# A hybrid encoder layer in fp32: a ring of its own for rows loaded ahead, and other ties for the loads of h

## The chip, the cores and the metric

The kernel runs on one core of a Trainium2 chip. Its engines work side by side: TensorE (PE) multiplies, VectorE (DVE), ScalarE (ACT) and GpSimd (POOL) do elementwise work, and SyncE (SP) issues every DMA of this kernel from one in-order queue. The metric is the device time of one execution in microseconds; the median of several runs counts. A lower time is better.

## The reference, cut to what matters

One layer of an encoder with two attention groups runs on 2048 prompt tokens and 32 sample tokens (a decoding step with 128 cached rows), D = 1024, all in fp32:

```
a  = rmsnorm(h)
qa, ka, va, qb, kb, vb = split(a @ w_in)
oa = diff_attn(qa, ka, va)            # 4 heads, two maps each, chunk-causal
ob = band_attn(qb, kb, vb)            # 8 heads of 64, a band of 9 chunks of 64
h  = h + concat(rmsnorm(oa), rmsnorm(ob)) @ w_out
h  = h + square(relu(rmsnorm(h) @ w_up)) @ w_down      # 4096 wide
h  = h + sigmoid(h @ w_ple_gate) * (p @ w_ple_proj)
y  = rmsnorm(h)
```

The outputs are y for both token sets and the new keys and values.

## The kernel before, in words

**Numbers.** Every operand of a product is split into a high and a low part (`split`, L232: ACT copies the high part as fp32r, POOL or DVE subtracts it from the raw value), and `mm3` (L257) makes each product of three matmuls: high x high (L267), high x low (L268), low x high (L269).

**Tokens.** There are four blocks `b` of 512 tokens; block 1 carries the 32 sample tokens as well. `HALVES` pairs the blocks (0, 1) and (2, 3). Between stages, activations lie in HBM: `oT` (attention outputs), `hS` (the residual stream h), `rB` (scales of a norm), `cB` (normed rows), `uS` (operands of the down product).

**Stages in `run` (L1482).** Projections and attention come first. The band attention's second half is followed in the program by `proj_a` (L1581), the projection of group A for blocks 2 and 3, woven by `weave2` (L131) with `onorm` (L840): for each of blocks 0 and 1, `onorm` loads the band outputs, sums their squares, and in a second step makes the norm's scale and stores it to `rB`. `ONP` (L119) says at which units of `proj_a` these two steps are taken: with (first, gap between the blocks, distance), block i steps at units first + i x gap and first + i x gap + distance. `proj_a` has 35 units, 0 to 34.

After that, `outproj` (L878) of blocks 0 and 1 runs. For each of eight column groups d it loads a row of x into a tile `hd`, multiplies, adds, squares it into a tile `tmp`, and stores the new h to `hS`. Woven into block 0's product is `oload(1)` (L853), which loads and splits the attention outputs of block 1 (tile `oraw`). Woven into block 1's product is `norms(0)` (L1603), which ends in `cnorm` (L921): it loads each row of h of block 0 from `hS` (tile `tmp`, by `cload`, L911) and splits it into `cH`, `cL`, the operands of the up product. All of `hd`, `tmp` and `oraw` have the tag `tmp` and share one ring of the pool `wk`, with 3 slots here (`nt`). The class `Mix` (L188) sends a tag to a pool of its own; `oload` and `outproj` load one row ahead when they are given a `Mix` (L862, L883).

The MLP of blocks 0 and 1 follows (`mlp`, L1003). For blocks 2 and 3 the up and down products are done by Strassen's scheme with seven products of half size: `uphase` (L1120) stores its results to `uS`; `dphase` (L1196) runs the seven down products `m` in the order 3, 5, 7, 4, 2, 6, 1. Each has eight steps `c` with two inner steps `k`. A step loads one or two tiles `wd` of w_down (a ring of 8) and a tile `ut` from `uS`, splits `ut` into two tiles `dx` (a ring of 4), makes sums `dv` of two weight tiles where the product wants one, and splits them into `dw`; twelve matmuls per `k` go to four tiles `dp` in PSUM. At the end of a product DVE adds `dp` into tiles of h in SBUF (L1249): product 3 adds into all eight parts of `h[3]`, product 5 into parts 0 to 3 of `h[2]` and `h[3]`. Into `dphase` are woven the gates of blocks 0 and 1 (`gate`, L1284), which load h of a block in one DMA, split it into `hH` and `hL`, load `pn` and gate weights into `wr`, and multiply (`gps`, `pps`).

**Ties.** The tiles h of blocks 2 and 3 (L1696) are loaded by `hmove` (L1622) from `hS` in parts of 128 x 512. So that these loads aren't issued at once, `hstep` (L1699) writes one column of each part from a `dx` tile; the load must wait for that write. `dphase` calls it as `step` (L1233).

**Order.** Each engine's instructions are put in order by a planner, which takes the program's order as priority and a model of the durations, and runs ahead with later instructions where earlier ones aren't ready in its model. On the chip the order is fixed and each engine goes through its own.

Of the kernel before, what the change touches and what calls it, by code (L numbers as in the profile page):

```python
# [12 lines left out]
F32 = mybir.dt.float32  # L13
F32R = mybir.dt.float32r
AF = mybir.ActivationFunctionType
# [29 lines left out]
HALVES = [(0, 1), (2, 3)]  # L45
# [68 lines left out]
OW = 1  # L114
# [1 line left out]
JA0 = [(0, 1), (2, 3, 8)]  # L116
JA1 = [(4, 5), (6, 7)]
JB = [(0, 1), (2, 3, 8), (4, 5), (6, 7)]
ONP = (16, 1, 6)  # L119
ONQ = (8, 1, 1)  # L120
PW = 256
GL = 3
# [4 lines left out]
def drain(gen):  # L127
    for _ in gen:
        pass


def weave2(main, sides, at):
    n = 0
    for _ in main:
        for i, side in enumerate(sides):
            if n in (at[0] + i * at[1], at[0] + i * at[1] + at[2]):
                next(side, None)
        n += 1
    for side in sides:
        drain(side)  # L140


def weave(main, side, step, i=0, n=1):
    for _ in main:
        if i % step == 0:
            for _ in range(n):
                next(side, None)
        i += 1
    drain(side)
# [47 lines left out]
class Kern:  # L197
# [998 lines left out]
    def dphase(self, h, pool, md, step):  # L1196
        nc = self.nc
        def wrow(q, c):
            i, j = int(q[0]) - 1, int(q[1]) - 1
            r = pool.tile([P, 2, 512], F32, tag="wd", bufs=6, name="wd")  # L1200
            self.dma(r.rearrange("p a b -> p (a b)"), self.a["w_down"][8 * j + c, i])
            return r

        def operands(m, sq, so, c):
            ws = [wrow(q, c) for q in sq]
            u = self.rawp.tile([P, 2, 512], F32, bufs=self.nraw, name="ut")
            self.dma(u, self.uS[:, m - 1, 2 * c : 2 * c + 2])
            for k in range(2):
                x = pool.tile([P, 2, 512], F32R, tag="dx", bufs=4, name="dx")
                self.tsplit(x, u[:, k], "dve")  # L1210
                v = ws[0][:, k]
                if len(ws) == 2:
                    v = pool.tile([P, 512], F32, tag="dv", bufs=4, name="dv")
                    nc.vector.tensor_tensor(v, ws[0][:, k], ws[1][:, k], op=so)
                w = self.wp.tile([P, 2, 512], F32R, tag="wc", bufs=self.wtags[2], name="dw")
                self.tsplit(w, v, "dve")
                yield w, x

        add, sub = ALU.add, ALU.subtract
        plan = [  # L1220
            (3, ("11",), add, (("12", add), ("22", add))),
            (5, ("11", "12"), add, (("11", sub), ("12", add))),
            (7, ("12", "22"), sub, (("11", add),)),
            (4, ("22",), add, (("11", add), ("21", add))),
            (2, ("21", "22"), add, (("21", add), ("22", sub))),
            (6, ("21", "11"), sub, (("22", add),)),
            (1, ("11", "22"), add, (("11", add), ("22", add))),
        ]
        for m, sq, so, outs in plan:
            ps = [md.tile([P, 512], F32, tag="mm", name="dp") for _ in range(4)]  # L1230
            for c in range(8):
                for k, (w, x) in enumerate(operands(m, sq, so, c)):
                    if m == 3 and k == 0:  # L1233
                        step(c, x)
                    for d in range(4):
                        sl = slice(P * d, P * d + P)
                        self.mm3(
                            ps[d], [(w[:, 0, sl], w[:, 1, sl], x[:, 0], x[:, 1])],
                            start=c + k == 0, stop=c == 7 and k == 1,
                        )  # L1240
                if c < 7:
                    yield
            adds = [(d, q, op) for d in range(4) for q, op in outs]
            if m == 1:
                adds.sort(key=lambda x: x[1])
            for d, q, op in adds:
                i, t = int(q[0]) - 1, int(q[1]) - 1
                hv = h[2 + t][4 * i + d]
                nc.vector.tensor_tensor(hv, hv, ps[d], op=op)  # L1249
            yield  # L1250
# [231 lines left out]
    def run(self):  # L1482
        tc, nc, a = self.tc, self.nc, self.a
        with ExitStack() as top:

            def opened(stack, name, bufs, space=None, side="left"):
                kw = {} if space is None else {"space": space}
                return stack.enter_context(
                    tc.tile_pool(name=name, bufs=bufs, side=side, reuse_waits="tile", **kw)
                )  # L1490
# [7 lines left out]
            mm = opened(psx, "mm", MM, PSUM)  # L1498
# [11 lines left out]
            with ExitStack() as x:  # L1510
# [10 lines left out]
                wk = opened(x, "setup", 1, side="right")  # L1521
# [59 lines left out]
            def proj_a():  # L1581
                yield from self.proj(HALVES[1], 0, acts, sg, mm, gs=range(GS))
                for b in HALVES[1]:
                    yield from self.proj((b,), 0, acts, sg, mm, vs=(), gs=range(GS, 4))

            weave2(proj_a(), [self.onorm(b, wq, mm, "mm", self.rB) for b in HALVES[0]], ONP)
            s12.close()
# [4 lines left out]
            oa = {}  # L1592
# [8 lines left out]
            wk = opened(sq_, "wk", 1)  # L1601
            acc, cn, st = {}, {}, {}
            def norms(b, act, ps):  # L1603
                r = self.colnorm(acc[b][0], b, 1.0 / D, wk, ps, "mm", None)
                yield
                yield from self.cnorm(b, wk, act, cn, r)

            acc = {b: [] for b in range(4)}
            with ExitStack() as x:
                oq = Sized(opened(x, "oq", 2), BLK, True)  # L1610
                weave(self.outproj(0, wk, oa[0], mm, acc[0]), self.oload(1, wk, oq, oa), 1, 0, OW)
                weave(self.outproj(1, wk, oa[1], mm, acc[1]), norms(0, actq, mm), 1, 1)
            hq = opened(sq_, "hq", 1)
            uq = Sized(opened(sq_, "uq", 10), BLK)
# [7 lines left out]
            def hmove(b, h, load, ds=range(8)):  # L1622
                for d in ds:
                    x, y = h[d][:, : BN[b]], self.hS[:, d, T0[b] : T0[b] + BN[b]]
                    self.dma(*((x, y) if load else (y, x)))
                return h
# [21 lines left out]
            for b in HALVES[0]:  # L1648
                if b == 1:
                    drain(self.cnorm(1, wk, actq, cn))  # L1650
                h = [hq.tile([P, BLK], F32, tag="h", bufs=8, name="h") for _ in range(8)]
                hmove(b, h, True)
                dn = Turn(mm)
                m = self.mlp(b, (h,) + cn[b], wk, uq, mm, dn, (16, 11)[b])
                if b == 0:
# [3 lines left out]
                    def steps(m=m):  # L1659
                        for ch, part in m:  # L1660
                            next(pre, None)
                            if part == 0:
                                yield ch

                    m = steps()
# [30 lines left out]
            h = {b: hh.tile([P, 8, 512], F32, tag="h", name="h") for b in HALVES[1]}  # L1696
            h = {b: [t[:, d] for d in range(8)] for b, t in h.items()}

            def hstep(c, x):  # L1699
                for b in HALVES[1] if c < 4 else ():  # L1700
                    for d in (2 * c, 2 * c + 1):
                        nc.gpsimd.tensor_copy(h[b][d][:, :1], x[:, 0, :1].bitcast(F32))
                    hmove(b, h[b], True, range(2 * c, 2 * c + 2))

            fk = opened(top, "fk", 1)
            udx, gqx = ExitStack(), ExitStack()
# [11 lines left out]
            for i, _ in enumerate(self.dphase(h, ud, md, hstep)):  # L1718
                if i == 48:
                    drain(g)  # L1720
                    gqx.close()
                    left = opened(top, "gx", 1)
                    pair = self.gatepair(h, t3, left, right, md, mg, GL)
                if pair is not None:
                    if 49 < i < 55:
                        next(pair)
                elif i % 4 != 3:
                    next(g, None)
# [68 lines left out]
```

## Time and profile before

| what | value |
|---|---|
| three runs | 2965.36, 2957.69, 2965.66 us |
| median | 2965.36 us |
| profiled execution | 2963.89 us, span 2962.1 us, mean granted clock 0.993 |
| HBM read, written | 443.81 MB, 131.22 MB |
| DMA over the span | 578.28 MB, mean 195 GB/s |

The span is the time from the first to the last instruction that the profiler records; the execution's time lies a little over it. An engine's busy time is the union of its instructions. Matmuls overlap in the array, so a matmul's own duration (0.40 us for 512 columns) is longer than the distance to the next one; distances are read from the starts. In rows of a timeline, "x4" is a group of four like instructions in a row, and a bracket tells how long the engine had been idle and which instruction ended it. "<-" reads "made from". "SPq" rows are issues of DMAs, not transfers.

### The profile page before, as it was taken

How to read it: one execution, taken by the hardware profiler on the slowest of the kernel's cores; microseconds unless marked ns; L12 is line 12 of the kernel's file. 1: busy time of each engine (PE TensorE's matmuls, PEld its weight loads, DVE VectorE, ACT ScalarE, POOL GpSimd, SP SyncE). 2: the span in 40 equal slices, each digit the busy share in tenths (PEclk: the TensorE clock that was granted, in tenths of full speed). 3: DMA queues.
4: the chain of work that ended last, by engine and by line, in shares of the span. 5: the costliest groups of instructions: out<-in, count | busy, mean ns of one | idle time of the engine just before them, and what ended most of it. 6: DMA issues, size and time to landing. Idle time of an engine off the chain costs nothing.

```text
span 2962.1 us, 49251 instructions
## 1 busy us (share of the span) xinstructions
PE 2899.6 (98%) x17041; PEld 2560.4 (86%) x17041; DVE 1754.8 (59%) x3930; ACT 1753.6 (59%) x3729; POOL 1349.1 (46%) x1863
## 2 busy tenths in 40 slices
PE   8999999999999999999999999999999989999998
PEld 7899888998889888888899999889788868888886
DVE  6566664444565543565766564447665656766965
ACT  5566666665666665766777675443545445555554
POOL 4675664333355555655455455440855533133000
PEclk9999999999999999999999999999999999999999
DMA  9975578766677544544743433566443495756811
GB/s 347 328 249 198 192 259 271 219 210 207 226 252 225 192 159 157 166 154 151 240 138 123 148 109 120 183 205 199 164 149 139 146 342 191 267 194 202 265 64 57
DMA packets 299785, 578.28 MB, mean 195 GB/s; under 512 B 34672, under 2 KB 132080, under 8 KB 299536
## 3 DMA queue, kind: packets, MB, share of 16 engines
q1 hardware_dynamic: 299536, 575.13, 58.3%
q8 instruction: 135, 2.21, 0.3%
q14 instruction: 114, 0.93, 0.1%
HBM read 443.81 MB, written 131.22 MB: 194 GB/s over the span
## 4 chain that ended last, share of the span: by engine, by line
PE 89%; DMA 5%; DVE 3%; ACT 2%; issue 1%; POOL 1%; SPq 0%; ACTq 0%; DVEq 0%; POOLq 0%
PE s L607 4%; PE ups L269 4%; PE ups L267 4%; PE ups L268 4%; PE dps L267 4%; PE dps L268 4%; PE dps L269 4%; PE qps L267 4%; PE qps L269 4%; PE qps L268 4%; PE xps L269 3%; PE xps L268 3%; PE xps L267 3%; PE dp L267 3%; PE dp L269 3%; PE dp L268 3%
## 5 line engine op out<-in xcount | busy, mean ns | idle before, releaser
L230 POOL TENSOR_TENSOR wl<-wr,wh 128x256 fp32r<-128x256 f32 x888 | 667.8, 783 | 703.2 <-ACT wh L235 583.2
L235 ACT ACTIVATE wh<-wr 128x1024 fp32r<-128x1024 f32 x258 | 272.5, 1056 | 214.4 <-PE dps L268 43.5
L267 PE MATMUL ups<-cH,wh 128*128 128x272 f32 (+1 forms) x768 | 249.9, 326 | 2.3 <-ACT cH L235 1.2
L267 PE MATMUL dps<-uh,wh 128*128 128x272 f32 (+1 forms) x768 | 250.5, 328 | 1.5 <-DVE h L1001 1.1
L269 PE MATMUL ups<-cH,wl 128*128 128x272 f32 (+1 forms) x768 | 249.7, 326 | 0.6 <-DVE wl L241 0.6
L268 PE MATMUL ups<-cL,wh 128*128 128x272 f32 (+1 forms) x768 | 249.6, 325 | 0.0
L268 PE MATMUL dps<-ul,wh 128*128 128x272 f32 (+1 forms) x768 | 248.7, 324 | 0.2 <-DVE ul L241 0.2
L269 PE MATMUL dps<-uh,wl 128*128 128x272 f32 (+1 forms) x768 | 247.9, 324 | 0.0
L267 PE MATMUL qps<-aH,wh 128*128 128x512 f32 (+3 forms) x640 | 228.8, 357 | 6.6 <-DVE qk L487 3.0
L269 PE MATMUL qps<-aH,wl 128*128 128x512 f32 (+3 forms) x640 | 227.4, 355 | 0.0
L268 PE MATMUL qps<-aL,wh 128*128 128x512 f32 (+3 forms) x640 | 226.8, 354 | 0.0
L268 PE MATMUL dp<-dx,dw 128*128 128x512 f32 x448 | 177.9, 397 | 0.0
L267 PE MATMUL dp<-dx,dw 128*128 128x512 f32 x448 | 168.1, 399 | 9.1 <-ACT dx L235 9.1
L269 PE MATMUL dp<-dx,dw 128*128 128x512 f32 x448 | 174.9, 397 | 0.0
L607 PE MATMUL s<-ka,q 128*128 128x512 f32 (+3 forms) x640 | 173.3, 368 | 0.5 <-DVE nm L616 0.4
L788 DVE CUSTOM_DVE_ANT_0 eb<-sb,bb 128x320 f32<-128x320 f32 (+2 forms) x232 | 104.1, 478 | 109.3 <-PE tpb L800 105.0
L613 DVE TENSOR_REDUCE nm<-s 128x1 f32<-128x512 f32 (+1 forms) x192 | 122.1, 641 | 77.8 <-PE s L607 76.0
L267 PEld LDWEIGHTS ups<-cH,wh 128*128 128x128 f32 x768 | 145.2, 189 | 15.2 <-ACT cH L235 1.5
L267 PEld LDWEIGHTS dps<-uh,wh 128*128 128x128 f32 x768 | 144.6, 189 | 14.0 <-DVE h L1001 2.6
L269 PEld LDWEIGHTS ups<-cH,wl 128*128 128x128 f32 x768 | 145.0, 189 | 11.9 <-DVE wl L241 1.0
L268 PEld LDWEIGHTS ups<-cL,wh 128*128 128x128 f32 x768 | 145.3, 189 | 11.6 <-DVE cL L241 0.4
L268 PEld LDWEIGHTS dps<-ul,wh 128*128 128x128 f32 x768 | 144.8, 189 | 10.6 <-DVE ul L241 0.4
(278 smaller groups left out, 8949.4 us busy)
## 6 DMA issues: line engine op xcount, KB each, us to landing
wd<-w_down SPq DMA_DIRECT2D x96, 512.0 KB, 5.2
q<-qS SPq DMA_DIRECT2D x128, 256.0 KB, 4.2
v<-vSa SPq DMA_DIRECT2D x64, 512.0 KB, 3.6
wr<-w_up SPq DMA_DIRECT2D x64, 512.0 KB, 3.8
wr<-w_down SPq DMA_DIRECT2D x64, 512.0 KB, 3.8
ut<-uS SPq DMA_DIRECT2D x56, 512.0 KB, 4.3
wr<-w_qk SPq DMA_DIRECT2D x54, 512.0 KB, 5.2
kS<-qk SPq DMA_DIRECT2D x32, 512.0 KB, 5.4
```

Of the source, the lines that this page charges most:

```text
L230: nc.gpsimd.tensor_tensor(out[:, sl], a[:, sl], b[:, sl], op=op)
L235: nc.scalar.activation(hi, raw, AF.Copy)
L267: nc.tensor.matmul(ps, lh, rh, start=start and i == 0, stop=False)
L268: nc.tensor.matmul(ps, lh, rl, start=False, stop=False)
L269: nc.tensor.matmul(ps, ll, rh, start=False, stop=stop and i == n - 1)
L607: nc.tensor.matmul(s, q[:, m, hl, P * qi : P * qi + nr], kt[:, m, k0 - kb : k0 - kb + n], start=hl == 0, stop=hl == 1)
L613: nc.vector.tensor_reduce(nmx, s, axis=AX.X, op=ALU.max, negate=True)
L788: nc.vector.tensor_tensor_reduce(e[:, w * i : w * i + w], s, bb[:nr, b0 + w * i : b0 + w * i + w], 1.0, -3e38, ALU.add, ALU.max, st[:, 3 + ...
```

## The change

Three things are edited. First, `ONP` becomes (17, 6, 7): block 0's steps move from units 16 and 22 to 17 and 24, block 1's from 17 and 23 to 23 and 30. Second, during the output products of blocks 0 and 1, `oload(1)` and `cnorm` of block 0 get a `Mix` that sends the tag `tmp` to a new pool `ot` with 2 slots; `oload(1)` thereby loads one row ahead, and `wk`'s ring of 3 is left to `outproj`. Third, `hstep` gets the number of the product. Before, POOL wrote the ties at steps 0 to 3 of the first product, two parts of each block per step (4 loads a step, 16 in all). Now ACT writes them: at steps 4 to 7 of the first product (m = 3) two parts of `h[3]` each, and at each step of the second product (m = 5) one part of `h[2]`.

```
-ONP = (16, 1, 6)
+ONP = (17, 6, 7)
...
             for c in range(8):
                 for k, (w, x) in enumerate(operands(m, sq, so, c)):
-                    if m == 3 and k == 0:
-                        step(c, x)
+                    if k == 0:
+                        step(m, c, x)
...
-                yield from self.cnorm(b, wk, act, cn, r)
+                yield from self.cnorm(b, wo, act, cn, r)
...
                 oq = Sized(opened(x, "oq", 2), BLK, True)
-                weave(self.outproj(0, wk, oa[0], mm, acc[0]), self.oload(1, wk, oq, oa), 1, 0, OW)
+                wo = Mix(wk, tmp=(opened(x, "ot", 1), 2))
+                weave(self.outproj(0, wk, oa[0], mm, acc[0]), self.oload(1, wo, oq, oa), 1, 0, OW)
                 weave(self.outproj(1, wk, oa[1], mm, acc[1]), norms(0, actq, mm), 1, 1)
...
-            def hstep(c, x):
-                for b in HALVES[1] if c < 4 else ():
-                    for d in (2 * c, 2 * c + 1):
-                        nc.gpsimd.tensor_copy(h[b][d][:, :1], x[:, 0, :1].bitcast(F32))
-                    hmove(b, h[b], True, range(2 * c, 2 * c + 2))
+            def hstep(m, c, x):
+                b, ds = {3: (3, range(2 * c - 8, 2 * c - 6) if c > 3 else ()), 5: (2, (c,))}.get(m, (2, ()))
+                for d in ds:
+                    nc.scalar.activation(h[b][d][:, :1], x[:, 0, :1].bitcast(F32), AF.Copy)
+                hmove(b, h[b], True, ds)
```

## The prediction

> **What bounds the kernel now.** I began with the page's head and its table of engines (engine, busy us and share of the span, number of instructions).
>
> ```profile
> span 2962.1 us, 49251 instructions
> PE 2899.6 (98%) x17041; PEld 2560.4 (86%) x17041; DVE 1754.8 (59%) x3930; ACT 1753.6 (59%) x3729; POOL 1349.1 (46%) x1863
> ```
>
> TensorE (PE) is busy for 98% of the span, and the change neither adds nor removes a matmul. So it can only move PE's idle time, 62.5 us in all, and the slow matmuls that follow a stop. The profiled execution took 2963.89 us, 1.5 under the median of the runs shown (2965.36); I make the sum on the span and carry the difference to the median.
>
> Next I went through PE's timeline for rows with an idle time ahead of them (in brackets: idle us and what ended it). The largest stops outside the first 15 us stand together, early in the first down product `dp`, where the diff moves the loads of `h`. Columns: start, duration, engine, line, operation, tiles.
>
> ```profile
> 2402.24 1.20 PE L267 MATMUL dp<-dx,dw 128*128 128x512 f32 x4 [0.72 <-ACT dx L235]
> ...
> 2404.92 0.40 PE L269 MATMUL dp<-dx,dw 128*128 128x512 f32 x1
> 2413.71 2.08 PE L267 MATMUL dp<-dx,dw 128*128 128x512 f32 x4 [8.40 <-ACT dx L235]
> 2415.59 0.63 PE L268 MATMUL dp<-dx,dw 128*128 128x512 f32 x1
> ...
> 2416.76 0.40 PE L269 MATMUL dp<-dx,dw 128*128 128x512 f32 x1
> ...
> 2428.70 0.39 PE L268 MATMUL dp<-dx,dw 128*128 128x512 f32 x1
> 2428.94 0.40 PE L269 MATMUL dp<-dx,dw 128*128 128x512 f32 x1
> 2433.09 0.51 PE L267 MATMUL gps<-hH,wh 128*128 128x512 f32 x1 [3.76 <-ACT wh L235]
> ...
> 2437.31 0.39 PE L269 MATMUL gps<-hH,wl 128*128 128x512 f32 x1
> ```
>
> Two stops, 8.40 and 3.76 us, with 0.72 ahead of them. Warm matmuls start 0.24 us apart (2428.70, 2428.94). From 2413.71 to 2416.76 seven starts take 3.05 us, so 3.05 - 7 x 0.24 = 1.37 us are lost to a slow clock; from 2433.09 to 2437.31 eleven take 4.22, so 1.58 are lost. The first stop costs 0.72 + 8.40 + 1.37 = 10.49 us in all, the second 3.76 + 1.58 = 5.34.
>
> What stood behind them I read from the timelines of ScalarE (ACT), GpSimd (POOL) and the DMA queue (SP).
>
> ```profile
> 2402.62 4.26 ACT L235 ACTIVATE hH<-h 128x512 fp32r<-128x512 f32 x8
> 2413.03 1.15 ACT L235 ACTIVATE dx<-ut 128x512 fp32r<-128x512 f32 x2 [6.16 <-POOL h L1702]
> ```
>
> ```profile
> 2403.31 8.75 POOL L220 TENSOR_TENSOR hL<-h,hH 128x256 fp32r<-128x256 f32 x8 [32.49 <-ACT hH L235]
> 2412.00 4.37 POOL L1702 COPY h<-dx 128x1 f32<-128x1 f32 x16
> ```
>
> ```profile
> 2404.84 8.59 SPq L211 DMA_DIRECT2D wd<-w_down  x6
> 2413.53 11.35 SPq L211 DMA_DIRECT2D h<-hS  x16
> 2425.24 0.56 SPq L211 DMA_DIRECT2D wr<-w_ple_proj  x1
> ```
>
> All sixteen POOL copies stand after POOL's low parts `hL` of the gate. Each reads the first `dx` of a step c = 0 to 3, and the ring of `dx` has four slots: with four unread tiles held, ACT cannot write a fifth. That is the 6.16 us, and behind it PE's 8.40. When the copies run, they release sixteen loads at once; SP issues them for 11.35 us, and the gate's weights come behind them. That is PE's second stop.
>
> The same stretch in windows (length, busy us of PE, PEld, DVE, ACT, POOL, granted clock, DMA share, GB/s) shows the clock down to 0.67 and the DMA engines full:
>
> ```profile
> 2410.00:2420.00 10.00, 6.29 (x21) 5.07 (x22) 7.11 (x10) 3.98 (x7) 6.37 (x18) 0.67 1.03 400
> 2420.00:2430.00 10.00, 9.34 (x40) 7.17 (x38) 0.00 (x0) 0.00 (x0) 0.00 (x0) 1.00 1.05 387
> ```
>
> **The change part by part.** *Loads of h.* The POOL copies go, and no step before c = 4 of the first product reads `dx` for a tie. So the first stop's cause goes: 10.49 us. PE would finish the rows that end at 2428.94 + 0.24 = 2429.18 at about 2418.7.
>
> What is late next is the gate's weights. Without the sixteen loads SP reaches them at 2413.53, not 2425.24: 11.71 us earlier. Moved by as much, the first gate matmul could start at 2433.09 - 11.71 = 2421.4, so 2.7 us of stop remain. I gain the smaller shift, 11.7 us, and the slow start after the second stop stays. If the weights came before PE did, the gain would be 10.49 + (2433.09 - 2429.18) + 1.58 = 16.0; that is the upper end.
>
> Whether a stop of 2.7 us still costs clock, the nearest stop tells, 2.34 us long in the attention stage:
>
> ```profile
> 1426.43 1.70 PE L682 MATMUL tpp<-ident,e 128*128 128x128 f32 x8 [2.34 <-DVE e L646]
> ```
>
> ```profile
> 1428.00:1430.00 2.00, 2.00 (x6) 1.58 (x6) 2.00 (x3) 2.00 (x5) 1.83 (x3) 0.50 0.70 262
> ```
>
> The clock was 0.50 after it, so I keep the 1.58 us as a cost. [...]
>
> The ties now cost ACT sixteen writes of one column. The nearest rows of ACT are its two-column operations:
>
> ```profile
> L277 ACT ACTIVATE rsy<-rsv 128x2 f32<-128x2 f32 x10 | 2.0, 201 | 0.1
> ```
>
> 16 x 0.20 = 3.2 us over two products, on an engine that in the windows above had over 6 of 10 us free: nothing on the path. Behind such a write stand the splits of `dx` and `dw`, and PE behind those. The write waits for the `dx` that ACT itself made just before, and for the memory that `h` takes over from the up phase; that is free once the last store from there has landed (chain of waits: start, duration, what):
>
> ```profile
> 2402.96 6.40 DMA uS<-u
> ```
>
> So at 2409.4. A tie for c = 4 that came right after the `hH` block (2402.62 + 4.26 = 2406.9) would hold ACT 2.5 us. By then PE has the eighth and ninth `dx` before it, 24 matmuls at 0.24 us or 5.8 us of work, which hide it. Bounds 0 to 2.5; I take 0.
>
> The loads themselves, in the table of DMA issues of this stretch (times, KB, median us to landing), and the two ends of their slack:
>
> ```profile
> h<-hS SPq DMA_DIRECT2D x16, 256.0 KB, 6.1
> ```
>
> ```profile
> 2436.28 1.15 ACT L235 ACTIVATE dx<-ut 128x512 fp32r<-128x512 f32 x2 [0.21 <-DMA ut<-uS]
> ```
>
> ```profile
> 2458.27 1.27 DVE L1249 TENSOR_TENSOR h<-h,dp 128x512 f32<-128x512 f32 x2
> ```
>
> The first product adds into all of `h[3]`, whose last pair is now tied to c = 7. The sixteenth `dx` was made by 2437.4, the first add came at 2458.27: 20.8 us. The pair needs 2 x 11.35 / 16 = 1.4 us of SP and 6.1 to land, 7.5 us. `h[2]` is first needed after the second product, and its loads come one per step. What they are moved past on SP are the loads of `ut` and `wd`; eight slots of `wd` cover them. Cost nothing; without that cover one landing, 6.1 us.
>
> *Own ring ahead of the output products.* Here the tiles of the chain show what shares a ring with what (chain of waits, then PE):
>
> ```profile
> 956.89 5.19 DMA hS<-hd
> 962.14 6.46 DMA tmp<-hS
> ```
>
> ```profile
> 970.10 0.73 PE L267 MATMUL ups<-cH,wh 128*128 128x512 f32 x2 [1.23 <-ACT cH L235]
> ```
>
> The last row of the norm could be loaded only when a store of the output product had left the shared slot, and PE stood 1.23 us for it. With a ring of two of its own the row comes earlier: 1.2 us gained. The other stops there are the band attention's own, and I leave them. Below nothing is possible, as the planner orders all engines anew: it is a rival.
>
> *Norm of the band outputs later.* Its steps go from units 16, 22 / 17, 23 of the projection to 17, 24 / 23, 30.
>
> ```profile
> 749.03 0.97 PE L785 MATMUL sb<-kbt,q 128*128 128x320 f32 x4 [0.57 <-DVE stb L788]
> ```
>
> ```profile
> 758.06 0.32 SPq L211 DMA_DIRECT2D rB<-r  x1
> ...
> 813.86 0.43 SPq L211 DMA_DIRECT2D rb<-rB  x1
> ```
>
> At most the 0.57 us go. The second scale is stored at 758.06 and read at 813.86; the eleven units between 23 and 34 fill that time at about 5 us each, so seven units later is 793, still 20 us ahead. Taken at nothing.
>
> Sum: 11.7 + 1.2 = 12.9 us. Span 2949.2, the profiled execution 2951.0, the median 2952.5.
>
> **Rivals.** *The wait stays, on VectorE.* PE needs the low part of `dx` as well:
>
> ```profile
> 2406.87 3.47 DVE L241 TENSOR_TENSOR hL<-h,hH 128x512 fp32r<-128x512 f32 x3
> 2410.26 2.34 DVE L1214 TENSOR_TENSOR dv<-wd 128x512 f32<-128x512 f32 x2
> 2413.69 1.31 DVE L241 TENSOR_TENSOR dx<-ut,dx 128x512 fp32r<-128x512 f32 x2 [1.09 <-ACT dx L235]
> ...
> 2447.31 0.69 DVE L1214 TENSOR_TENSOR dv<-wd 128x512 f32<-128x512 f32 x1
> ```
>
> If DVE keeps its order, `dx` is made at 2412.6 + 0.65 = 2413.3, and PE's first matmul on a low part (2415.59) moves by 2.3 us only. PE then meets the gate's weights ready, which saves 5.5: 7.8 + 1.2 = 9.0, median 2956.4. For it: beside POOL's `hL` a `dv` takes 1.17 us, alone 0.69. Against it: `dv` serves the second product, and stood ahead only as `dx` was blocked. [...]
>
> *h comes late.* If the last pair is tied less than 7.5 us ahead of the adds, VectorE waits in order, the splits behind it too, and PE up to a landing and a slow start, 6.1 + 1.4 = 7.5: gain 5.4, median 2960.
>
> *Slower: the own ring lets rows into the band attention.* Sixteen rows (eight of the load, eight of the norm) can now be split earlier, on the ACT and DVE that band attention waits for. Each one put ahead of a softmax step costs PE a stop like that at 970.10 and a slow start, 1.23 + 1.37 = 2.6 us. From eight rows on (20.8 against 11.7 + 8.9) it is slower; all sixteen give 41.6 - 11.7 = 30 more, median 2995. Against it: the rows' work is the same, and PE has output products to fill in.
>
> **How the numbers follow.** Forecast, with its upper end, 0.62; wait on VectorE 0.16; h late 0.10; slower 0.12. About 0.3% (8.9 us) is what a measurement here can tell from no change; the border is 2956.5. VectorE's case lies on it and is halved: faster 0.62 + 0.08 = 0.70, same 0.08 + 0.10 = 0.18, slower 0.12. The range goes from the upper end (16.0 + 1.2 + 0.57, 2947.6), less 4 for the runs' spread of 8 us, to the late h at 2960 and 3 over: 2944 to 2963. The forecast's own range is 2947 to 2956.
>
> **What would show it.** Right: no POOL copy of `h`; no PE row near 2405 waiting for `dx` for over 2 us; the loads of `h` in pairs among `ut` and `wd` and then singly; the gate's weights issued some 11 us earlier; the row into `cH` without a store ahead of it. Wrong: DVE's `dx` behind `hL` and `dv`, with PE waiting on it; a DVE add waiting for `h<-hS`; new PE stops on `stb` or `pHb` between 813 and 1000.

## The result and the profile after

The changed kernel takes 2936.14 us (median of 4 runs, 2935.13 to 2941.41); the kernel before took 2963.16 on the same chip (4 runs, 2957.69 to 2965.66). The ratio, taken over all runs, is 0.9914 [0.9898, 0.9931], a gain of 25 us (0.86%); the two medians lie 27.0 us apart. The direction was forecast. The size was not: 12.9 us were forecast, and the measured time lies below the range of 2944 to 2963.

The profiled execution after took 2941.41 us. The head of its page:

```profile
span 2939.6 us, 49272 instructions
PE 2893.5 (98%) x17041; PEld 2558.0 (87%) x17041; DVE 1754.2 (60%) x3930; ACT 1756.6 (60%) x3745; POOL 1348.1 (46%) x1847
```

PE is idle for 46.1 us of the span; before it was 62.5. The sixteen ties moved from POOL (1863 to 1847) to ACT (3729 to 3745). Two places changed.

**The first down product.** PE's timeline has no row with an idle time between 2380 and 2440. The windows (length, busy us of PE, PEld, DVE, ACT, POOL, granted clock, DMA share, GB/s):

```profile
2400.00:2410.00 10.00, 10.00 (x44) 8.08 (x43) 10.00 (x10) 5.41 (x13) 8.50 (x8) 1.00 1.04 407
2410.00:2420.00 10.00, 10.00 (x44) 8.08 (x43) 3.86 (x5) 3.74 (x8) 6.75 (x8) 1.00 1.03 404
2420.00:2430.00 10.00, 10.00 (x44) 8.09 (x43) 8.71 (x14) 7.19 (x16) 0.00 (x0) 1.00 0.83 306
```

PE is busy for all of it at full clock; between 2400 and 2420 us the DMA engines are as full (shares 1.04 and 1.03) as they were behind the stops of the kernel before (1.03 and 1.05). ACT's timeline, and under it SP's queue:

```profile
2396.76 4.26 ACT L235 ACTIVATE hH<-h 128x512 fp32r<-128x512 f32 x8
2400.93 1.14 ACT L235 ACTIVATE dx<-ut 128x512 fp32r<-128x512 f32 x2
...
2404.58 0.48 ACT L1703 ACTIVATE h<-dx 128x1 f32<-128x1 f32 x4 [1.47 <-DMA wr<-w_ple_proj]
```

```profile
2398.14 0.32 SPq L211 DMA_DIRECT2D uS<-u  x1
2398.80 0.56 SPq L211 DMA_DIRECT2D wr<-w_ple_proj  x1
2399.44 0.76 SPq L211 DMA_DIRECT2D wd<-w_down  x1
2400.75 0.44 SPq L211 DMA_DIRECT2D wr<-w_ple_gate  x1
2402.01 1.67 SPq L211 DMA_DIRECT2D wd<-w_down  x3
...
2411.27 1.80 SPq L211 DMA_DIRECT2D h<-hS  x4
```

ACT makes two `dx` right behind the `hH` block; before, it stood 6.16 us at that place. The first four ties take it 0.48 us, behind 1.47 us of idle time. PE does not stop for them. SP issues the first of the gate's weights straight behind the last store of `uS`, 12.5 us ahead of the first tied loads of `h`; before, they came behind all sixteen.

**Output products within band attention.** The profile before shows nine stops between 740 and 1000 us, six of them from 884 on. Two of the six, beside the one at 970.10:

```profile
886.26 0.56 PE L785 MATMUL sb<-kbt,q 128*128 128x320 f32 x2 [1.32 <-DVE stb L788]
...
977.02 0.63 PE L800 MATMUL tpb<-ident,eb 128*128 128x128 f32 x4 [0.97 <-DVE pLb L810]
```

In the changed kernel all stops from 884 on are gone, and so is the one at 749. What is left stands between 820 and 841 us, six stops of 2.3 us in all (PE's timeline):

```profile
820.00 0.97 PE L785 MATMUL sb<-kbt,q 128*128 128x320 f32 x4 [0.36 <-DVE stb L788]
...
831.94 0.51 PE L268 MATMUL ops<-oact,wh 128*128 128x512 f32 x1 [1.02 <-DVE oact L241]
```

To see where the time came from, PE's idle time and its time lost to a slow clock are added up from windows of 20 us laid over the whole span, by stage (idle + clock, us). Lost to the clock is an estimate: PE's busy time in a window times what the granted clock lacks of 1.00 (behind the two stops of the third row it gives 3.3, the distances of the starts 1.37 + 1.58 = 2.95); idle time at a low clock counts once, as idle.

| stage | before | after |
|---|---|---|
| to 740 us | 22.9 + 3.3 | 24.8 + 8.1 |
| 740 to 2060 (bands, A, first MLP) | 12.7 + 6.6 | 7.5 + 0.0 |
| 2060 to 2440 (up phase, first down product) | 13.3 + 3.3 | 0.4 + 0.0 |
| from 2440 on | 13.6 + 1.6 | 13.4 + 1.7 |

The change took 11.8 us from the second row and 16.2 from the third. The first row is the spread of executions, since PE runs the same instructions in the same order there: the profiled execution after lost 6.7 us more, and is 5 us above its median.

### The profile page after: what moved, and what is told of

It is laid out like the page before. It is cut to its first block, busy times and chain, and to the rows that moved or that the text cites. A ratio compares the mean times of both kernels' runs of the same rounds, so it can differ in the third digit from the quotient of the medians.

```text
span 2939.6 us, 49272 instructions
## 1 busy us (share of the span) xinstructions
PE 2893.5 (98%) x17041; PEld 2558.0 (87%) x17041; DVE 1754.2 (60%) x3930; ACT 1756.6 (60%) x3745; POOL 1348.1 (46%) x1847
## 4 chain that ended last, share of the span: by engine, by line
PE 89%; DMA 5%; DVE 3%; ACT 1%; issue 1%; POOL 0%; SPq 0%; ACTq 0%; DVEq 0%; POOLq 0%
PE s L607 4%; PE ups L269 4%; PE ups L268 4%; PE ups L267 4%; PE dps L267 4%; PE dps L269 4%; PE dps L268 4%; PE qps L267 4%; PE dp L267 4%; PE dp L268 4%; PE dp L269 4%; PE qps L268 4%; PE qps L269 4%; PE xps L269 3%; PE xps L268 3%; PE xps L267 3%
## 5 line engine op out<-in xcount | busy, mean ns | idle before, releaser
L267 PEld LDWEIGHTS ups<-cH,wh 128*128 128x128 f32 x768 | 144.6, 188 | 13.4 <-ACT wh L235 1.2
L267 PEld LDWEIGHTS dps<-uh,wh 128*128 128x128 f32 x768 | 144.3, 188 | 13.6 <-DVE h L1001 2.5
L269 PEld LDWEIGHTS ups<-cH,wl 128*128 128x128 f32 x768 | 144.5, 188 | 11.8 <-DVE wl L241 0.9
L267 PE MATMUL vps<-wh,aH 128*128 128x256 f32 (+1 forms) x528 | 151.0, 288 | 3.2 <-ACT vraw L446 3.2
```

The source lines that it names most:

```text
L267: nc.tensor.matmul(ps, lh, rh, start=start and i == 0, stop=False)
L269: nc.tensor.matmul(ps, ll, rh, start=False, stop=stop and i == n - 1)
```

## The experiments

Ratios are to the kernel before, run on the same chip (medians 2957.2 to 2958.8 us), with 95% intervals; a ratio r is turned into us as (1 - r) x 2958.

### The three edits, one at a time

**a_only** has only the first edit (`ONP`), **b_only** only the second (the own ring), **c_only** only the third (the ties); **bc** has the second and the third.

> The kernel before with the first edit alone (steps of the band norm at units 17, 24 and 23, 30). Theory: nothing beyond 3 us either way, as forecast, since at most the stop of 0.57 us at 749 us hangs on it. Rival: a plan with later steps gains 5 us or more, by moving the norm's vector work away from band attention's.

> The kernel before with the second edit alone (own ring of two slots and a row ahead). Theory: this edit carries most of what the output products' stage gained, 8 to 12 us, by taking the stops of 0.3 to 1.3 us and the slow clock after them out of 813 to 980 us. Rival: it takes only the one stop of 1.23 us ahead of the up product (the forecast's 1.2 us), and the rest comes from the first edit.

> The kernel before with the third edit alone (ties of h by ScalarE at the later steps). Theory: the two stops of TensorE at the start of the first down product (16.0 us with their slow starts) are all that this edit touches, so it gives 15 to 18 us against before and the stage from 740 to 1000 us stays as it was, with its stops. Rival: the earlier stage's gain depends on none of the edits alone, and this edit gives less than 12 us, as forecast, with a stop left ahead of the gate's first product.

> The whole change without its first edit (the norm's steps stay at 16, 22 and 17, 23). Theory: the three edits add up, so this is 2 to 4 us slower than the whole change and 22 to 25 us faster than before. Rival: the norm's place matters only in the plan without the own ring, and this is as fast as the whole change (27 us) or faster.

| run | median us | ratio | gain |
|---|---|---|---|
| a_only | 2957.03 | 0.9989 [0.9980, 0.9998] | 3.3 |
| b_only | 2952.06 | 0.9974 [0.9966, 0.9983] | 7.7 |
| c_only | 2943.61 | 0.9944 [0.9931, 0.9957] | 16.6 |
| bc | 2937.80 | 0.9931 [0.9919, 0.9944] | 20.4 |

Within the intervals the edits add up: 3.3 + 7.7 + 16.6 = 27.6 against 25.4 for all. c_only came as expected; b_only and bc fell a little short of their ranges (8 to 12, 22 to 25). c_only has no PE stop in the first down product, and keeps stops from 884 on; with b_only it is the other way round, but for one new stop of 0.41 us at 923. So the two places belong to the two edits. `ONP` alone is worth something between 0.6 and 5.9 us, barely clear of noise, and no view shows where: in a_only the 0.57 us stop at 749 is gone, and PE's idle time from 740 to 1000 is 7.3 us against 6.9 before.

### The ties: engine, step or memory?

The forecast put the first stop down to GpSimd's order: copies behind `hL`, with `dx` held. The rival is that no engine could have written the ties earlier, since the memory of `h` still belonged to the up phase. Three kernels tell these apart. **c_act_early** leaves the ties at steps 0 to 3 and changes only the engine:

```
-                        nc.gpsimd.tensor_copy(h[b][d][:, :1], x[:, 0, :1].bitcast(F32))
+                        nc.scalar.activation(h[b][d][:, :1], x[:, 0, :1].bitcast(F32), AF.Copy)
```

> The kernel before with the ties of h written by ScalarE, but at the old steps 0 to 3 of the first product and for both blocks, sixteen loads. Theory of the forecast (GpSimd's order holds the ties): the first stop goes with the change of engine, 10 us gained, and the sixteen loads still stand ahead of the gate's weights, so the second stop stays. Rival (the memory of h is free only when the up phase's last stores have landed, so that any tie of steps 0 to 3 holds a slot of dx until then, whichever engine writes it): the first stop of 8 us stays, and the time is within 3 us of before or slower, as ScalarE itself now waits.

Measured: 2958.02 us, ratio 1.0006 [0.9996, 1.0015], no gain. ACT's timeline, then PE's:

```profile
2395.95 4.26 ACT L235 ACTIVATE hH<-h 128x512 fp32r<-128x512 f32 x8
2402.96 1.60 ACT L1702 ACTIVATE h<-dx 128x1 f32<-128x1 f32 x16 [2.75 <-DMA pn<-pT]
2404.47 1.65 ACT L235 ACTIVATE dx<-ut 128x512 fp32r<-128x512 f32 x3
```

```profile
2405.14 2.08 PE L267 MATMUL dp<-dx,dw 128*128 128x512 f32 x4 [6.48 <-ACT dx L235]
2426.59 0.80 PE L267 MATMUL gps<-hH,wh 128*128 128x512 f32 x1 [4.89 <-ACT wh L235]
```

ACT stands 2.75 us idle and then writes all sixteen at once. The profile names `pn<-pT` as the last to end; the tie doesn't read `pn`. The last store of `uS` was issued at 2396.63 and landed 6.2 us later by the table of DMA issues, at 2402.8; the ties begin at 2402.96. So the memory held them. GpSimd's order was worth 8.40 - 6.48 = 1.9 us of the first stop, and the second stop, 4.89 for 3.76, took 1.1 of them back.

**c_pool_late** is the third edit with the copies left on GpSimd; **c_act_late16** ties all sixteen parts on ACT at steps 4 to 7 of the first product. Both are told against the changed `hstep`; the other two edits are left out.

```
-                    nc.scalar.activation(h[b][d][:, :1], x[:, 0, :1].bitcast(F32), AF.Copy)
+                    nc.gpsimd.tensor_copy(h[b][d][:, :1], x[:, 0, :1].bitcast(F32))
```

```
-                b, ds = {3: (3, range(2 * c - 8, 2 * c - 6) if c > 3 else ()), 5: (2, (c,))}.get(m, (2, ()))
+                ds = range(2 * c - 8, 2 * c - 6) if m == 3 and c > 3 else ()
+                for b in HALVES[1]:
...
```

> The kernel before with the ties still written by GpSimd, but at the later steps (h[3] at steps 4 to 7 of the first product, h[2] in the second). Theory now (a tie can't be written before the memory of h is free, when the up phase's last stores have landed, so what matters is the step and not the engine): as good as the edit with ScalarE, 14 to 18 us faster than before, no stop of over 2 us in the first product. Rival (GpSimd's order behind its low parts of the gate holds the ties): a stop of 3 to 8 us for dx stays near 2405 us and the gain is under 10 us.

> The kernel before with ScalarE's ties at steps 4 to 7 of the first product for both blocks: four loads a step, sixteen in the first product, none in the second. Theory: the first stop goes as with the whole edit, as no tie of steps 0 to 3 is left; the gate's weights are planned ahead of the loads, so the second goes too: 13 to 17 us faster, and putting h[2] in the second product is worth under 3 us. Rival (sixteen loads in one product hold up the queue): a stop of 3 us or more ahead of the gate's product or at the end of the first down product, and a gain of under 12 us.

Measured: 2942.73 and 2942.72 us, both 0.9948 (to 0.9962 and 0.9960), 15.4 us: with GpSimd or ACT, with eight loads in this product or sixteen, the gain of c_only within its interval. What counts is the step. In c_act_late16 the wait is seen in the open:

```profile
2407.87 0.86 ACT L1703 ACTIVATE h<-dx 128x1 f32<-128x1 f32 x8 [2.57 <-DMA uS<-u]
```

ACT waits 2.57 us for the store of `uS` to land, the bound of 2.5 that the forecast gave this tie, and PE, as forecast, has work enough: no stop.

**c_mem_right** keeps the old ties, and gives `h` memory on the side that the up phase's operands have left:

```
-            hh = opened(top, "hh", 2)
+            hh = opened(top, "hh", 2, side="right")
```

> The kernel before with its old ties (GpSimd, steps 0 to 3, sixteen loads), but the pool of h opened on the other side, so that h takes the memory of the up phase's operands, which TensorE has read by 2384 us, and not that of the tiles whose stores land at 2409 us. Theory (memory of h holds the ties): the copies run near 2385 us, the stop of 8.4 us for dx goes, and what is left depends on the sixteen loads, which now compete earlier with the weights: 5 to 16 us faster. Rival (the step or the engine itself is what matters): the stop for dx stays within 2 us of its 8.4 us.

Measured: 2951.76 us, 0.9976 [0.9967, 0.9985], 7.1 us. POOL's timeline, then PE's:

```profile
2378.33 0.54 POOL L1702 COPY h<-dx 128x1 f32<-128x1 f32 x4 [12.65 <-ACT dx L235]
...
2388.74 7.58 POOL L1702 COPY h<-dx 128x1 f32<-128x1 f32 x4 [3.26 <-ACT dx L235]
```

```profile
2416.72 1.83 PE L267 MATMUL dp<-dx,dw 128*128 128x512 f32 x4 [3.47 <-ACT dx L235]
2427.20 0.74 PE L267 MATMUL gps<-hH,wh 128*128 128x512 f32 x1 [3.03 <-ACT hH L235]
```

With other memory, the same copies on the same engine run from 2378 on instead of at 2412, ahead of `hL` and not behind it, and the 8.4 us stop is gone. So the copies' place behind `hL` followed from the memory as well. With c_act_early, where another engine waited for the same memory, that settles the cause. But more than half of c_only's gain is not there: the sixteen loads of 256 KB now go out from 2378.55 on, while the stores of `uS` and the loads of `wd` fill the DMA engines (share 1.03), and two other stops of 3 us come in. The late steps avoid both.

### The second stop: where the gate's weights wait

Their raw tiles `wr` and `pn` share a ring of four with `ut`, and a `ut` is released when it is split into `dx`. So blocked `dx` should also keep the weights from being loaded. **c_graw2** keeps the old ties, and gives the gate's raw tiles two slots of their own; for the memory the ring of `wd` goes from 8 to 6, and **c_wd6**, the control, has that alone.

```
-        raw = self.rawp.tile([P] + shape, F32, bufs=self.nraw, name="wr")
+        raw = (self.graw or self.rawp).tile([P] + shape, F32, bufs=2 if self.graw else self.nraw, name="wr")
...
+            self.graw = Rings((opened(gqx, "gw", 1), "wr"))
...
```

> Control for the next run: the kernel before with the ring of w_down tiles cut from 8 to 6 slots, which makes room for a ring of the gate's own. Theory: the two stops early in the first down product stay as they are (8.4 and some 3.8 us) and the time is within 3 us of before. Rival: the cut ring itself moves the gate's weights ahead and takes the second stop away.

> The kernel of the control with a ring of two slots for the raw tiles of the gates of blocks 0 and 1 alone, which before shared four slots with the down product's operand ut. The old ties stay, and so does the first stop. Theory (the gate's weights were late as their slot came free only when a dx was split, behind the first stop): they are now issued before the sixteen loads of h, and the second stop of 3.8 us and its slow start go; 3 to 6 us faster than the control. Rival (the weights were late only as they are planned behind the loads in the queue): the second stop stays.

Measured: c_wd6 2954.25 us, 0.9987 [0.9978, 0.9996]; c_graw2 2953.36, 0.9980 [0.9971, 0.9989]. In time the two can't be told apart (3 to 6 us were expected between them); the stops can be. c_wd6 and c_graw2, PE's timelines:

```profile
2399.80 1.20 PE L267 MATMUL dp<-dx,dw 128*128 128x512 f32 x4 [2.59 <-ACT dx L235]
...
2425.78 0.79 PE L267 MATMUL gps<-hH,wh 128*128 128x512 f32 x1 [5.42 <-ACT wh L235]
```

```profile
2398.73 1.21 PE L268 MATMUL dp<-dx,dw 128*128 128x512 f32 x4 [0.72 <-ACT dx L236]
2409.47 2.07 PE L268 MATMUL dp<-dx,dw 128*128 128x512 f32 x4 [7.66 <-ACT dx L236]
```

With slots of their own the weights are issued ahead of the loads, and PE's stop at `gps` is gone, while the first stop stays. The control is not quite the kernel before, against what was expected of it: its first stop is split into three, of 2.59, 0.57 and 0.86 us, and its second has grown to 5.42. All its stops here come to 9.4 us, those of c_graw2 to 8.4: what the second gave, the first took back, and so the time hardly moves. SP's queue in c_graw2:

```profile
2380.99 0.64 SPq L212 DMA_DIRECT2D wr<-w_ple_proj  x1
...
2404.43 0.33 SPq L212 DMA_DIRECT2D wr<-w_ple_gate  x1
...
2408.43 7.82 SPq L212 DMA_DIRECT2D h<-hS  x8
```

So the second stop hung on ring slots as well. In the changed kernel the weights go ahead of the loads without a ring of their own; that this is because `dx` isn't held and the slots of `ut` come free is the reading of these runs, not a test of its own.

### The own ring: a row ahead, an order, or slots?

The second edit does three things: one row more is loaded ahead, the rows no longer queue behind `hd` and its stores, and there are 3 + 2 slots for 3. **b_noahead** leaves the row ahead out (a subclass of `Mix`, for which `oload` has `ahead` = 0).

```
+class Own(Mix):
+    pass
...
+                wo = Own(wk, tmp=(opened(x, "ot", 1), 2))
...
```

> The kernel before with the own ring of two slots for the rows of the load and of the norm, but no row loaded ahead. Theory: the ring is what counts (a row no longer waits for a store or a square of the output product to leave its slot), so nearly all of the edit's 7.7 us stay: 5 to 9 us. Rival: the row ahead is what counts, and under 3 us are left.

Measured: 2952.40 us, 0.9976 [0.9967, 0.9986], 7.1 us: the row ahead is worth nothing that can be seen.

For slots against order, **b_shared5** gives one shared ring five slots in a new pool, **b_nt4** gives the old ring a fourth slot (`self.nt, self.nr = 4, 1`), and **ot3** is the changed kernel with three slots in the own ring.

> The kernel before with one ring of five slots for all the rows of this stage (hd, tmp, rows of the load and of the norm), nothing loaded ahead: the slots of the old ring and of the new one together, but shared. Theory (what counts is that the two chains don't take turns on the same slots): under half of the gain of the own ring, 0 to 4 us faster than before. Rival (what counts is the number of slots): as good as the own ring, 6 to 9 us.

> The shared ring of the kernel before gets a fourth slot in its own pool wk (3 to 4), so the memory is where it was; no ring of its own, no row ahead, no other edit. Theory that the number of slots is what edit two brings: most of its 7.7 us come, 4 to 8 us, and of the stops between 813 and 980 us those at 886 and 945 and the 1.23 us one at 970 shrink as they did with the own ring. Rival, that it matters that the rows of the norm and of the load don't queue behind stores of the output product (order of the ring, not its length): a fourth slot only shifts the order by one, 0 to 3 us are gained, and a stop of about 1.2 us in the norm's rows stays with a store of hS ahead of it in the chain.

> The changed kernel with three slots in the own ring where it has two. If slots are still short after the change, the stops left between 813 and 850 us (0.36, 0.18, 0.26, 1.02, 0.27, 0.17 us) shrink and 1 to 3 us are gained on the changed kernel: ratio to the kernel before 0.990 to 0.991. If two are enough, it equals the changed kernel within 0.1%: ratio 0.9914, the same stops.

Measured: 3310.48 us, 1.1201 [1.1186, 1.1217]; 3261.20 us, 1.1024 [1.1002, 1.1047]; 3284.81 us, 1.1102 [1.1087, 1.1117]. None of the three expectations had that. PE's groups from 1000 to 1400 us, during the attention of group A, in the kernel before and in b_nt4 (operation, count, busy us, mean ns, idle time ahead and what ended it):

```profile
L267 PE MATMUL dps<-uh,wh 128*128 128x512 f32 x222 | 88.8, 400 | 0.0
...
L267 PE MATMUL ups<-cH,wh 128*128 128x512 f32 x202 | 80.1, 396 | 0.0
...
L607 PE MATMUL s<-ka,q 128*128 128x512 f32 (+1 forms) x154 | 42.7, 372 | 0.0
```

```profile
L607 PE MATMUL s<-ka,q 128*128 128x512 f32 (+1 forms) x340 | 116.4, 462 | 45.0 <-ACT e L620 25.6 <-DMA q<-qS 9.6 <-DVE nm L616 8.5
L682 PE MATMUL tpp<-ident,e 128*128 128x128 f32 x284 | 55.9, 342 | 48.2 <-DVE e L646 48.1
```

In the kernel before, up and down products of the MLP (`ups`, `dps`) fill PE while the attention's softmax runs. In b_nt4 not one of them lies in these 400 us (nor in b_shared5 and ot3): the attention runs alone, PE waits for the softmax, and the granted clock falls to 0.78 (1200 to 1400 us). One slot is 544 columns of fp32, 2.2 KB per partition. The reading is that it pushed the pools behind it, the MLP's, into memory that the attention holds until it ends. These runs alone don't prove that, and say nothing of slots against order.

The next pair puts it to the test. **b_ring5** moves the tag `tmp` out of `wk` for this stage only, into one shared ring of five slots, and opens a ring of three in its place behind the stage, so that the pools that follow lie where they lay. **b_ring3** is the control, with three.

```
+                wo = Own(wk, tmp=(opened(x, "wt", 1), 5))
...
+            wk = Own(wk, tmp=(opened(sq_, "wt", 1), 3))
```

> Only the stage of the first output products is changed: the tag tmp leaves wk, and all of hd, tmp and oraw share one ring of five slots in a pool that is open for this stage alone; behind it a ring of three is opened again in its place, so the pools that follow lie where they lay. Five slots as in the changed kernel (3 + 2), but in one order. Theory that the number of slots counts: the same gain as the own ring, 5 to 9 us, and the stops at 886, 945 and 970 us go. Rival, that the separate order counts: 0 to 3 us and the 1.2 us stop of the norm's last row stays. If the memory moves after all, output or up products are missing between 1000 and 1500 us as in the two slow ones and the run tells nothing.

> The control for the run with five shared slots: the same pools, with three slots in the stage's ring as in the kernel before. By both theories within 2 us of the kernel before, since slots and order are the same and only the pool's name differs; what it shows beyond that is the price of handing the memory over.

Measured: b_ring5 2953.77 us, 0.9989 [0.9980, 0.9997]; b_ring3 2961.13 us, 1.0013 [1.0005, 1.0022]. Five slots instead of three, in one order, with the MLP's memory in place: no collapse, which bears out the reading of the three slow runs, and 2961.13 - 2953.77 = 7.4 us, as much as the own ring gave. So more slots are enough for a gain of that size. The comparison rests on the control, which is itself 3.9 us slower than the kernel before for a reason that I haven't traced; against the kernel before, b_ring5 gains 3.4 us, between the 5 to 9 expected for slots and the 0 to 3 for order. PE's timeline in b_ring3, and the one stop at the first of these places in b_ring5:

```profile
884.71 0.38 PE L830 MATMUL ob<-pHb,vbt 128*128 128x256 f32 x1 [0.43 <-ACT pHb L813]
886.24 0.56 PE L789 MATMUL sb<-kbt,q 128*128 128x320 f32 x2 [1.15 <-DVE stb L792]
...
966.24 0.74 PE L271 MATMUL ups<-cH,wh 128*128 128x512 f32 x2 [0.65 <-ACT cH L239]
973.16 0.63 PE L804 MATMUL tpb<-ident,eb 128*128 128x128 f32 x4 [0.96 <-DVE pLb L814]
```

```profile
884.52 0.39 PE L830 MATMUL ob<-pHb,vbt 128*128 128x256 f32 x1 [0.20 <-ACT pHb L813]
```

Of the stops that name the softmax of band attention (`stb`, `pHb`, `pLb`), those at 886 and 973 go with the slots and the one at 884.71 shrinks; three new ones of about 0.3 us each come in at 965 to 967. PE's idle time from 740 to 1000 us falls from 5.4 to 3.4, so 2.0 us of the gain are seen there; the rest these two profiles do not locate. What the slots change is when the rows of the norm are split into `cH` (the view of that tile: count, shortest/median/longest ns, first to last start; b_ring3, b_ring5, b_only):

```profile
L239 ACT ACTIVATE cH<-tmp x8: 614/632/637, 902.8 to 965.6; 128x512 fp32r<-128x512 f32 x8
L239 ACT ACTIVATE cH<-tmp x8: 631/632/633, 900.1 to 955.0; 128x512 fp32r<-128x512 f32 x8
L235 ACT ACTIVATE cH<-tmp x8: 616/631/633, 894.3 to 924.4; 128x512 fp32r<-128x512 f32 x8
```

With five shared slots the last row comes 10.6 us earlier, with the own ring 41 us. So order counts for the rows, though no run shows that it counts for the time. The reading is that the softmax was not at fault: too little other work was ready for PE in the gaps.

No run's median beat the changed kernel's.

## Why the prediction was right in sign and wrong in size

- **First stop, 10.49 us: right in size, wrong in cause.** The step that failed: "All sixteen POOL copies stand after POOL's low parts `hL` of the gate." They did, but that was worth 1.9 us; the rest was the memory of `h`. The prediction had the row for it, the store that lands at 2409.4, and used it only to price the new tie. The effect was right since the edit moved the ties to steps near that landing, and let go of `dx` before it. The forecast did not reckon with this; that the size came out was luck.
- **Second stop: the step that failed.** "Moved by as much, the first gate matmul could start at 2433.09 - 11.71 = 2421.4, so 2.7 us of stop remain" took SP's order for fixed but for the missing loads. The weights' place in it hung on ring slots too: with slots of their own they went ahead of the same loads (c_graw2). In the changed kernel they are issued at 2398.80, not 2413.53, and the stop goes with its slow clock. The upper end written beside the forecast, 16.0, is what the edit brought: 16.6 (c_only), 15.4 (two variants). 11.7 was forecast for this term; some 4 to 5 us of the miss are here.
- **Own ring, 1.2 us: the other failed step.** "The other stops there are the band attention's own, and I leave them." Measured 7.7 and 7.1; 6 us of the miss. The idle times ahead of `stb`, `pHb`, `pLb` and `hd` at 884 to 977 us, 4.5 us with the 1.23, went together, one of them with a slow clock behind that cost 1.6 us in the profile before. They name the engine that ended the wait; that more slots for the rows took most of them away says that other work was missing. How much of the gain is slots and how much the separate order stays open.
- **`ONP`, nothing:** measured 3.3 [0.6, 5.9]. The cause stays open.
- **The rivals.** VectorE's order didn't hold PE: its `dx` follows `hL` directly, at 2404.48, and there is no stop. `h` wasn't late. The slower rival had a wrong mechanism, rows put ahead of a softmax step, which no run shows. A real one was near and unseen: one slot more, and the kernel is 10% slower.

## What to carry to other kernels

In these runs a write into a new tile waited for the last user of the memory under it (in c_act_early the store landed at 2402.8 us and the ties began at 2402.96), and the `dx` that it read stayed held meanwhile (PE stood 6.48 us for the next): before blaming the engine in whose queue the write stands, ask when the memory comes free, and follow the held slots through every ring that they feed. An idle time names the instruction that ended it, not the work that could have filled it; where independent work is woven into a latency-bound stage, the ring that feeds this work can set the stops (five slots for three took PE's idle time from 740 to 1000 us from 5.4 to 3.4 us). One slot more made this kernel 10% slower (b_nt4), by the reading above as it shifted the pools that are opened later: after such an edit, look first whether the stages still overlap.

## What the hardware showed unexpectedly

Behind a stop of about 1 us the granted clock was 0.50 in one profile and 1.00 in another. In the kernel before and in b_ring3 PE stands at the same instruction, for 1.32 and 1.15 us. The window behind it, before and then b_ring3:

```profile
888.00:890.00 2.00, 2.00 (x11) 2.00 (x11) 0.28 (x3) 0.92 (x2) 0.00 (x0) 0.50 0.63 250
```

```profile
888.00:890.00 2.00, 1.90 (x17) 1.71 (x17) 0.86 (x5) 1.78 (x4) 0.00 (x0) 1.00 0.66 264
```

The small difference in length does not explain it. Some 70 us earlier both stand for 0.59 and 1.00 us ahead of the same instructions, and from 816 to 818 the clock is 0.50 in the kernel before and 1.00 in b_ring3; b_noahead, with the same two stops, has 0.50. Over 740 to 1500 us the kernel before lost 4.9 us to the clock in three drops, the third behind the stop of 2.34 us at 1426; b_ring3 lost none, with 1.64 us at that place. In the first row of the table by stage PE runs the same instructions in the same order, and lost 3.3 us to the clock before and 8.1 after. So some of the 6.6 us of clock in its second row may be that of the one execution, and the medians are the better measure of the edit. What decides whether the clock drops behind such a stop, no run here shows.
